# Sums of squares for the norms: four tiles added on GpSimd before TensorE sums the partitions, and a last block that ends tile by tile

## The chip, the cores and the metric

One core of a Trainium2 chip runs the whole program. The metric is device time in microseconds (us) of one execution; a lower number is better. The engines are named as in the profile: PE (TensorE), DVE (VectorE), ACT (ScalarE), POOL (GpSimd), SP (which issues DMAs).

## What is computed

The reference is two transformer blocks over 256 tokens of width 1024, all in fp32. The first mixes by grouped-query attention and a long convolution and then runs a product-key mixture of experts; the second group has four feed-forward blocks, two attentions (one differential, one with forget gates) and a key/value stage. What matters here is the norm that stands ahead of each stage:

```python
def rmsnorm(x, g):
    xf = x.astype(jnp.float32)
    y = xf * lax.rsqrt(jnp.mean(xf * xf, axis=-1, keepdims=True) + EPS)
    return (y * g.astype(jnp.float32)).astype(x.dtype)
```

The result of the last block goes through one more such norm, and that is the output.

## The kernel before

The activations stay in SBUF transposed: X is eight tiles of 128 features x 256 tokens in fp32, features on the partitions. Weights come from HBM as 427 loads of 1 MB, called raw, issued by SP into a ring of five buffers (three in the early stages). Each raw holds two units of 128 x 1024. ACT copies a unit to a reduced format (whi, about 1.06 us) and DVE subtracts to get the rest (wlo, about 1.22 us); the split units stand in a second ring of five buffers (LOOK + 1 = 3 in the early stages, XLOOK = 2 more later). PE multiplies a unit by the hi and lo parts of the activations, 24 matmuls in all (hi x whi, hi x wlo, lo x whi for eight tiles).

The stages run in the order mix, peer, f00, diff, f01, kv, f10, forget, f11. A norm needs the sum of squares over the features, that is over tiles and partitions: ACT squares each of the eight tiles (sq), and PE multiplies each square by a matrix of ones and accumulates eight products in one PSUM tile, ss. These matmuls are fp32; each shows in the profile as two rows. ACT then takes the root (r0, with a table load ahead of it where the function on ACT changes) and DVE the reciprocal (rstd).

In the stages from peer on, `norm_begin` doesn't wait for rstd: it scales X by the gain alone (xg, hi parts on ACT and lo parts on DVE), PE multiplies the first units by xg (outputs qkv, gux, kvu, bq, wq), and `fixed` multiplies their PSUM results by rstd afterwards (fix, DVE). A unit's PSUM buffer is free only after its fix, so PE can run three units (u1, u2, u3 below) and has to wait with the fourth (u4) for the fix of u1. In f00 two norms are merged: that of the first part's end and that of f00. So ss has two halves there; the second is weighted with the square of the gain `fin` (tile fsq).

`rstd` is the plain form, used twice in mix (for X and for the context). `finish` is the end of f11: eight updates of X by DVE, a square of each (six on ACT, two on DVE), eight ss matmuls, root, reciprocal, eight products, four output DMAs. Ahead of it `out_tiles` multiplies the last two pairs of f11 into eight output tiles, held in four PSUM tiles acc0 to acc3.

Python order, priorities and a list scheduler set the order of each engine's instructions when the program is built; on the chip each engine runs its list in order and waits at an instruction until its inputs are there. GpSimd has little to do: fills, index patterns and five DMA issues, among them that of scr<-vec, a 1.5 MB scatter of a bias table to HBM in f00 (`diff_setup`: PE's bv, ACT's vec, then POOL's DMA).

Everything is recorded by one helper, so that the profile shows nearly all instructions at L263; tiles tell them apart.

Of the kernel before, what the change touches and what calls it, by code (L numbers as in the profile page):

```python
# [9 lines left out]
F32 = mybir.dt.float32  # L10
# [117 lines left out]
PACE = {"route": {"v": 1}, "kv_norm": {"v": 2}}  # L128
NOSYNC = mybir.DependencyInfo(mybir.DependencyClass.NoSync, mybir.DependencyReason.DATA)
# [152 lines left out]
class Kern:  # L282
# [160 lines left out]
    def rstd(self, x, pool, n=D, tag="rstd"):  # L443
# [5 lines left out]
        for kt in range(nk):  # L449
            sq = pool.tile([P, T], F32, tag="sq", name="sq", bufs=3)  # L450
            nc.scalar.activation(sq, x[:, kt], AF.Square)
            nc.tensor.matmul(ps, self.ones, sq, start=kt == 0, stop=kt == nk - 1)
# [4 lines left out]
        return o  # L457

# [9 lines left out]
    def norm_begin(self, pool, G, sh, xg, fin=None, psq=None):  # L468
# [22 lines left out]
        fsq = None  # L491
        if fin is not None:
            fsq = pool.tile([P, KT], F32, tag="fsq", name="fsq", bufs=1)
            nc.vector.tensor_mul(fsq, fin, fin)
        for kt in range(KT):
            sq = (psq or pool).tile([P, T], F32, tag="sq", name="sq", bufs=8 if psq else 4)
            nc.scalar.activation(sq, x[:, kt], AF.Square)
            for j in range(n):
                w = fsq[:, kt:kt + 1].to_broadcast([P, P]) if j else self.ones
                nc.tensor.matmul(ps[:, j], w, sq, start=kt == 0 and j == 0, stop=kt == KT - 1, skip_group_check=n > 1)  # L500
# [65 lines left out]
    def ffn(self, ph, l, i):  # L566
# [7 lines left out]
        with ExitStack() as es:  # L574
# [20 lines left out]

            def out_tiles():
                ws = [S.take(ph, self.ffn_order("o", f)) for f, _, _ in pend]
                self.rows(acc, [(f, w, (ah, al)) for w, (f, ah, al) in zip(ws, pend)], NF)
                pend.clear()
                self.tick()  # L600

            for f in range(NF):
# [38 lines left out]
                pend.append((f, ah, al))  # L641
            out_tiles()
# [3 lines left out]
            if ph == "f11":  # L646
                self.finish(pa, pn, parts, half)
            else:
                self.add_x(parts, half)
# [12 lines left out]
    def finish(self, psq, pool, parts, g):  # L662

        nc = self.nc
        ps = self.ps_bg.tile([P, T], F32, tag="bg", name="ss")
        for kt, p in enumerate(parts):
# [3 lines left out]
            if kt < 6:  # L670
                nc.scalar.activation(sq, x, AF.Square)
            else:
                nc.vector.tensor_mul(sq, x, x)
            if kt == 5:
                nc.scalar.activation(pool.tile([P, 1], F32, tag="sqw", name="sqw", bufs=1), self.eps, AF.Sqrt)
            nc.tensor.matmul(ps, self.ones, sq, start=kt == 0, stop=kt == KT - 1)
# [1354 lines left out]
```

## Time and profile before

| what | value |
|---|---|
| median of 3 runs | 2221.97 us (2220.69 to 2222.41) |
| profiled execution | 2221.92 us, span 2220.1 us |
| PE / DVE / ACT / POOL busy | 98% / 77% / 52% / 0% of the span |
| granted TensorE clock, mean | 0.995 |
| chain that ended last | PE 86%, DVE 8%, ACT 3%, DMA 3% |
| matmuls into ss | 88, shown as 176 rows |

The span is what the profiler saw of the program; 1.8 us of the execution lie around it. The chain is followed back from the last instruction to what released each, so its shares say which engine the end of the program hangs on.

### The profile page before, as it was taken

Reading aid. Unit: us, or ns where it says so; the run is one execution under the profiler, and the core shown is the slowest. Engines: PE = TensorE matmul, PEld = TensorE weight load, DVE = VectorE, ACT = ScalarE, POOL = GpSimd, SP = SyncE. Lnnn points to the kernel's source line nnn. Section 1 sums busy time; section 2 is a strip of 40 time slices with the busy share of each in tenths; the row PEclk is TensorE's granted clock in tenths of the full one; section 3 lists DMA queues with packets and bytes.
Section 4 is the critical chain, followed back from the end, with each engine's and each line's share of the span. In section 5 each row is a group of like instructions: output and inputs, shape, how many; then the busy total and the mean of one; then the engine's idle time right before and its main releaser. Section 6 shows DMA issues by size and latency. Waiting matters only on the chain.

```text
span 2220.1 us, 41653 instructions
## 1 busy us (share of the span) xinstructions
PE 2176.8 (98%) x17298; PEld 2091.2 (94%) x17298; DVE 1706.2 (77%) x3056; ACT 1150.0 (52%) x1788; POOL 10.9 (0%) x25
## 2 busy tenths in 40 slices
PE   7999999999999999999999899999999999999998
PEld 4887999999889999999999899999999999999998
DVE  7789689887996777567777687878776887798554
ACT  5677565454334444444455345766445544476443
POOL 0000000000000000000000000000000000000000
PEclk9999999999999999999999999999999999999999
DMA  8256344544349888557776875436784688724551
GB/s 317 77 188 221 126 180 152 190 176 185 124 152 274 303 304 297 198 204 271 291 286 193 323 307 225 146 141 225 299 305 165 228 323 313 273 96 171 190 180 49
DMA packets 100605, 481.20 MB, mean 217 GB/s; under 512 B 40808, under 2 KB 41336, under 8 KB 44928
## 3 DMA queue, kind: packets, MB, share of 16 engines
q1 hardware_dynamic: 95744, 462.70, 57.4%
q10 hardware_dynamic: 3456, 10.90, 1.3%
q0 software_dynamic: 1216, 4.94, 1.0%
q8 instruction: 136, 2.23, 0.4%
q14 instruction: 53, 0.43, 0.1%
HBM read 467.48 MB, written 11.03 MB: 216 GB/s over the span
## 4 chain that ended last, share of the span: by engine, by line
PE 86%; DVE 8%; ACT 3%; DMA 3%; issue 1%; SPq 0%; DVEq 0%; ACTq 0%
PE acc L263 27%; PE gu L263 19%; PE u L263 15%; PE win L263 4%; DMA raw<-wts 3%; PE qkv L263 2%; PE gux L263 2%; DVE wlo L263 2%; PE pacc L263 2%; PE kvu L263 2%; PE gps L263 2%; PE ss L263 2%; PE sc L263 1%; DVE A L263 1%; PE po L263 1%; ACT whi L263 1%
## 5 line engine op out<-in xcount | busy, mean ns | idle before, releaser
L263 DVE TENSOR_TENSOR wlo<-raw,whi 128x1024 fp32r<-128x1024 f32 x650 | 792.6, 1222 | 302.8 <-ACT whi L263 301.0
L263 ACT ACTIVATE whi<-raw 128x1024 fp32r<-128x1024 f32 x650 | 684.3, 1055 | 498.2 <-PE acc L263 128.1
L263 PE MATMUL gu<-hh,wlo 128*128 128x256 f32 x1264 | 309.9, 283 | 0.0
L263 PE MATMUL gu<-hh,whi 128*128 128x256 f32 x1264 | 309.8, 283 | 0.0
L263 PE MATMUL acc<-wh,whi 128*128 128x256 f32 x1024 | 289.8, 283 | 0.0
L263 PE MATMUL acc<-wh,wlo 128*128 128x256 f32 x1024 | 289.8, 283 | 0.0
L263 PE MATMUL acc<-wl,whi 128*128 128x256 f32 x1024 | 289.8, 283 | 0.0
L263 DVE SCALAR_TENSOR_TENSOR junk<-raw,crow 128x1024 f32<-128x1024 f32 x198 | 241.7, 1220 | 47.4 <-DMA raw<-wts 38.6
L263 PE MATMUL u<-hh,whi 128*128 128x256 f32 x1024 | 253.7, 284 | 3.4 <-ACT whi L263 3.4
L263 PE MATMUL u<-hh,wlo 128*128 128x256 f32 x1024 | 253.1, 285 | 2.1 <-DVE wlo L263 2.1
L263 PEld LDWEIGHTS gu<-hh,whi 128*128 128x128 f32 x1264 | 241.5, 191 | 0.0
L263 PEld LDWEIGHTS gu<-hh,wlo 128*128 128x128 f32 x1264 | 241.5, 191 | 0.0
L263 PE MATMUL acc<-ah,whi 128*128 128x256 f32 x704 | 198.5, 282 | 6.7 <-ACT ah L263 6.7
L263 PEld LDWEIGHTS u<-hh,whi 128*128 128x128 f32 x1024 | 196.4, 192 | 5.1 <-ACT whi L263 5.1
L263 PEld LDWEIGHTS u<-hh,wlo 128*128 128x128 f32 x1024 | 196.2, 192 | 5.2 <-DVE wlo L263 4.0
L263 PE MATMUL acc<-al,whi 128*128 128x256 f32 x704 | 198.7, 283 | 0.8 <-DVE al L263 0.8
L263 PE MATMUL acc<-ah,wlo 128*128 128x256 f32 x704 | 197.0, 280 | 0.0
L263 PEld LDWEIGHTS acc<-wh,whi 128*128 128x128 f32 x1024 | 196.6, 192 | 0.0
L263 PEld LDWEIGHTS acc<-wh,wlo 128*128 128x128 f32 x1024 | 196.6, 192 | 0.0
L263 PEld LDWEIGHTS acc<-wl,whi 128*128 128x128 f32 x1024 | 196.6, 192 | 0.0
L263 PE MATMUL gu<-hl,whi 128*128 128x256 f32 x1264 | 177.4, 283 | 0.0
L263 PEld LDWEIGHTS gu<-hl,whi 128*128 128x128 f32 x1264 | 163.0, 191 | 0.0
(393 smaller groups left out, 4034.2 us busy)
## 6 DMA issues: line engine op xcount, KB each, us to landing
raw<-wts SPq DMA_DIRECT2D x427, 1024.0 KB, 4.9
G<-sp ACTq DMA_DIRECT2D x16, 512.0 KB, 2.6
gl<-G SPq DMA_DIRECT2D x16, 512.0 KB, 7.0
Fb<-fscr POOLq DMA_DIRECT2D x1, 2048.0 KB, 9.5
scr<-vec POOLq DMA_DIRECT2D x1, 1536.0 KB, 36.9
KR<-wts SPq DMA_DIRECT2D x1, 1024.0 KB, 11.1
KS<-wts SPq DMA_DIRECT2D x1, 1024.0 KB, 12.8
X<-xT SPq DMA_DIRECT2D x1, 1024.0 KB, 14.8
```

What stands on the lines that cost most here:

```text
L263: i = f(*a, **kw)
```

## The change

The sum of squares gets a method of its own, `sumsq`. ACT squares the eight tiles as before. GpSimd adds pairs of squares and then the two sums, so that four tiles become one in three additions, and PE multiplies only that one by the ones: two matmuls for eight tiles and six additions on GpSimd, where eight matmuls stood. It is used by both calls of `rstd` (four buffers for squares instead of three) and by `norm_begin` (five instead of four). In f00 the second half of ss has eight squares of its own, taken by ACT with the gain as a scale, and fsq goes. Over the program 60 matmuls go, 60 additions on GpSimd and eight squares on ACT come.

The second part concerns the end of f11: `out_last` multiplies both remaining pairs into one output tile, then both into the next, and `finish` becomes a generator that updates X two tiles at a time behind them and issues the ss matmuls of a pair of tiles after the next pair. There all eight ss matmuls stay on PE.

```diff
--- before.py
+++ after.py
@@ -126,6 +126,8 @@
 CH = 4
 
 PACE = {"route": {"v": 1}, "kv_norm": {"v": 2}}
+
+SQB = 5
 NOSYNC = mybir.DependencyInfo(mybir.DependencyClass.NoSync, mybir.DependencyReason.DATA)
 ASTEPS, HSTEPS = 1.5, 1
 RRATE = 60
@@ -446,15 +448,26 @@
         ps = self.ps_bg.tile([P, T], F32, tag="bg", name="ss")
         nk = n // P
         nc.scalar.activation(pool.tile([P, 1], F32, tag="sqw", name="sqw"), self.eps, AF.Sqrt)
-        for kt in range(nk):
-            sq = pool.tile([P, T], F32, tag="sq", name="sq", bufs=3)
-            nc.scalar.activation(sq, x[:, kt], AF.Square)
-            nc.tensor.matmul(ps, self.ones, sq, start=kt == 0, stop=kt == nk - 1)
+        self.sumsq(pool, ps, x, nk)
         r = pool.tile([P, T], F32, tag="r0", name="r0", bufs=1)
         nc.scalar.activation(r, ps, AF.Sqrt, scale=1.0 / n, bias=self.eps)
         o = pool.tile([P, T], F32, tag=tag, name=tag)
         nc.vector.reciprocal(o, r)
         return o
+
+    def sumsq(self, pool, ps, x, nk=KT, start=True, scale=None, bufs=4, **kw):
+
+        nc = self.nc
+        sq = []
+        for kt in range(nk):
+            t = pool.tile([P, T], F32, tag="sq", name="sq", bufs=bufs)
+            nc.scalar.activation(t, x[:, kt], AF.Square, scale=1.0 if scale is None else scale[:, kt:kt + 1])
+            sq.append(t)
+            if kt % 2:
+                nc.gpsimd.tensor_add(sq[kt - 1], sq[kt - 1], t)
+            if kt % 4 == 3:
+                nc.gpsimd.tensor_add(sq[kt - 3], sq[kt - 3], sq[kt - 1])
+                nc.tensor.matmul(ps, self.ones, sq[kt - 3], start=start and kt == 3, stop=kt == nk - 1, **kw)
 
     def mod_args(self, sh, sc, g, i=0):
         self.S.flush_ada([sh, sc])
@@ -488,16 +501,9 @@
                 nc.scalar.activation(hi[:, kt, :T], x[:, kt], AF.Copy, scale=Gx[:, kt:kt + 1])
                 nc.vector.scalar_tensor_tensor(lo[:, kt, :T], x[:, kt], Gx[:, kt:kt + 1], hi[:, kt, :T],
                                                op0=ALU.mult, op1=ALU.subtract)
-        fsq = None
-        if fin is not None:
-            fsq = pool.tile([P, KT], F32, tag="fsq", name="fsq", bufs=1)
-            nc.vector.tensor_mul(fsq, fin, fin)
-        for kt in range(KT):
-            sq = (psq or pool).tile([P, T], F32, tag="sq", name="sq", bufs=8 if psq else 4)
-            nc.scalar.activation(sq, x[:, kt], AF.Square)
-            for j in range(n):
-                w = fsq[:, kt:kt + 1].to_broadcast([P, P]) if j else self.ones
-                nc.tensor.matmul(ps[:, j], w, sq, start=kt == 0 and j == 0, stop=kt == KT - 1, skip_group_check=n > 1)
+        for j in range(n):
+            self.sumsq(psq or pool, ps[:, j], x, start=j == 0, scale=fin if j else None, bufs=8 if psq else SQB,
+                       skip_group_check=n > 1)
         r = pool.tile([P, T], F32, tag="rstd", name="rstd", bufs=1)
         r0 = pool.tile([P, T], F32, tag="r0", name="r0", bufs=1)
         with self.tc.high_priority(offset=NPRIO):
@@ -592,6 +598,20 @@
                     nc.vector.scalar_tensor_tensor(self.X[:, kt], self.X[:, kt], fin[:, kt:kt + 1], rf,
                                                    op0=ALU.mult, op1=ALU.mult)
                     yield
+
+            def out_last():
+
+                ws = [S.take(ph, self.ffn_order("o", f)) for f, _, _ in pend]
+                fin = self.finish(pa, pn, [acc[o // 2][:, o % 2] for o in range(8)], self.half(self.ada_done[mods[2]]))
+                for o in range(8):
+                    s = slice(o * P, (o + 1) * P)
+                    for w, (f, ah, al) in zip(ws, pend):
+                        self.mm_unit(acc[o // 2][:, o % 2], (w[0][:, s], w[1][:, s]), (ah, al), kts=range(1),
+                                     start=False, stop=f == NF - 1, skip_group_check=True)
+                    if o % 2:
+                        next(fin)
+                for _ in fin:
+                    pass
 
             def out_tiles():
                 ws = [S.take(ph, self.ffn_order("o", f)) for f, _, _ in pend]
@@ -639,14 +659,15 @@
                 if pend and f < NF - 1:
                     out_tiles()
                 pend.append((f, ah, al))
+            if ph == "f11":
+                assert mods[2] in self.ada_done
+                out_last()
+                return
             out_tiles()
             S.flush_ada(mods[2:]) if mods[2] not in self.ada_done else None
             self.mark("ffn.fin")
             parts, half = [acc[o // 2][:, o % 2] for o in range(8)], self.half(self.ada_done[mods[2]])
-            if ph == "f11":
-                self.finish(pa, pn, parts, half)
-            else:
-                self.add_x(parts, half)
+            self.add_x(parts, half)
 
     @staticmethod
     def ffn_order(kind, f):
@@ -663,6 +684,11 @@
 
         nc = self.nc
         ps = self.ps_bg.tile([P, T], F32, tag="bg", name="ss")
+        sqs = []
+
+        def ss(kt):
+            nc.tensor.matmul(ps, self.ones, sqs[kt], start=kt == 0, stop=kt == KT - 1)
+
         for kt, p in enumerate(parts):
             x = self.X[:, kt]
             nc.vector.scalar_tensor_tensor(x, p, g[:, kt:kt + 1], x, op0=ALU.mult, op1=ALU.add)
@@ -671,9 +697,15 @@
                 nc.scalar.activation(sq, x, AF.Square)
             else:
                 nc.vector.tensor_mul(sq, x, x)
+            sqs.append(sq)
             if kt == 5:
                 nc.scalar.activation(pool.tile([P, 1], F32, tag="sqw", name="sqw", bufs=1), self.eps, AF.Sqrt)
-            nc.tensor.matmul(ps, self.ones, sq, start=kt == 0, stop=kt == KT - 1)
+            if kt % 2:
+                for k in range(kt - 3, kt - 1) if kt >= 3 else ():
+                    ss(k)
+                yield
+        ss(KT - 2)
+        ss(KT - 1)
         r0 = pool.tile([P, T], F32, tag="r0", name="r0", bufs=1)
         nc.scalar.activation(r0, ps, AF.Sqrt, scale=1.0 / D, bias=self.eps)
         r = pool.tile([P, T], F32, tag="rstd", name="rstd", bufs=1)
```

Where the lists of the engines change most, with buffer numbers in the names:

First ACT at the norm of f00, before: splits of units (whi), the root r0, and rf, a second root that is used later.

```order
834 L263 ACTIVATE whi_13251<-raw_13042 128x1024
835 L263 ACTIVATE whi_13285<-raw_13042 128x1024
836 L263 ACTIVATE r0_13220<-ms2_13223 128x256
837 L263 ACTIVATE whi_13335<-raw_13105 128x1024
838 L263 ACTIVATE rf_13582<-ms_13221 128x256
839 L263 ACT_TABLE_LOAD
```

And after, from the last of the sixteen squares on (cols_76 holds the gain):

```order
843 L265 ACTIVATE sq_13228<-X_80,cols_76 128x256
844 L265 ACTIVATE whi_13265<-raw_13042 128x1024
845 L265 ACTIVATE whi_13299<-raw_13042 128x1024
846 L265 ACTIVATE whi_13349<-raw_13105 128x1024
847 L265 ACTIVATE whi_13391<-raw_13105 128x1024
848 L265 ACTIVATE r0_13234<-ms2_13237 128x256
849 L265 ACTIVATE vec_13480<-bv_13478 8x384
```

Two more splits stand ahead of r0, the fourth of them being whi_13391; vec, which scr's DMA waits for, has moved from behind several later instructions to the place after r0.

Second PE at the norm of diff, before: six of the eight ss matmuls stand together inside the first unit, qkv_15635 (x8 are its lo products); qkv_15672 is u2.

```order
8961 L263 MATMUL qkv_15635<-xg0_13152,wlo_15429 128x258
8962 L263 MATMUL ss_15569<-sq_15594,ones_78 128x256
8963 L263 MATMUL ss_15569<-sq_15597,ones_78 128x256
8964 L263 MATMUL ss_15569<-sq_15600,ones_78 128x256
8965 L263 MATMUL ss_15569<-sq_15603,ones_78 128x256
8966 L263 MATMUL ss_15569<-sq_15606,ones_78 128x256
8967 L263 MATMUL ss_15569<-sq_15609,ones_78 128x256
8968 L263 MATMUL qkv_15635<-xg1_13153,whi_15428 128x258 x8
8969 L263 MATMUL qkv_15672<-xg0_13152,whi_15456 128x258
```

And after, where qkv_15649 is u1 and qkv_15686 is u2 (whi_15470 and wlo_15471 come from the same raw as those of u1). The first ss stands after 31 products of the two units, the second after 38, with ten of u2 behind it:

```order
8955 L265 MATMUL qkv_15686<-xg0_13152,whi_15470 128x258
8956 L265 MATMUL ss_15583<-sq_15602,ones_78 128x256
8957 L265 MATMUL qkv_15649<-xg1_13153,whi_15442 128x258 x3
8958 L265 MATMUL qkv_15686<-xg0_13152,wlo_15471 128x258
8959 L265 MATMUL qkv_15686<-xg0_13152,whi_15470 128x258
8960 L265 MATMUL qkv_15686<-xg0_13152,wlo_15471 128x258
8961 L265 MATMUL qkv_15649<-xg1_13153,whi_15442 128x258
8962 L265 MATMUL ss_15583<-sq_15614,ones_78 128x256
8963 L265 MATMUL qkv_15686<-xg0_13152,whi_15470 128x258
8964 L265 MATMUL qkv_15686<-xg0_13152,wlo_15471 128x258
8965 L265 MATMUL qkv_15686<-xg1_13153,whi_15470 128x258 x8
8966 L265 MATMUL qkv_15721<-xg0_13152,whi_15506 128x258
```

The two units are interleaved now, and the two ss stand within them, each waiting for GpSimd.

Third ACT at the norm of diff, before and after. From the third square on before:

```order
962 L263 ACTIVATE sq_15594<-X_80 128x256
963 L263 ACTIVATE sq_15597<-X_80 128x256
964 L263 ACTIVATE sq_15600<-X_80 128x256
965 L263 ACTIVATE sq_15603<-X_80 128x256
966 L263 ACTIVATE sq_15606<-X_80 128x256
967 L263 ACTIVATE sq_15609<-X_80 128x256
968 L263 ACTIVATE whi_15631<-raw_15268 128x1024
969 L263 ACT_TABLE_LOAD
970 L263 ACTIVATE r0_15613<-ss_15569,eps_83 128x256
971 L263 ACTIVATE whi_15666<-raw_15268 128x1024
```

From the fifth square on after:

```order
974 L265 ACTIVATE sq_15614<-X_80 128x256
975 L265 ACTIVATE sq_15616<-X_80 128x256
976 L265 ACTIVATE sq_15619<-X_80 128x256
977 L265 ACTIVATE sq_15621<-X_80 128x256
978 L265 ACTIVATE whi_15645<-raw_15282 128x1024
979 L265 ACTIVATE whi_15680<-raw_15282 128x1024
980 L265 ACT_TABLE_LOAD
981 L265 ACTIVATE r0_15627<-ss_15583,eps_83 128x256
982 L265 ACTIVATE whi_15717<-raw_15349 128x1024
```

Both splits of the next raw now stand ahead of the table load and r0. On DVE, behind r0 in both orders, come the reciprocal, one wlo and the fix of u1.

## Rows read from the trace of the kernel before

**Rows 1.** The page, part 1: busy time of each engine over the span.

```profile
PE 2176.8 (98%) x17298; PEld 2091.2 (94%) x17298; DVE 1706.2 (77%) x3056; ACT 1150.0 (52%) x1788; POOL 10.9 (0%) x25
```

**Rows 2.** Windows: length, busy us (instructions) by engine, PE clock, DMA share, GB/s.

```profile
40.00:60.00 20.00, 18.31 (x118) 16.46 (x117) 19.44 (x41) 13.28 (x24) 0.00 (x0) 0.91 0.70 265
...
320.00:340.00 20.00, 20.00 (x171) 20.00 (x170) 20.00 (x85) 12.17 (x21) 0.00 (x0) 1.00 0.44 158
...
1520.00:1540.00 20.00, 20.00 (x170) 20.00 (x170) 18.50 (x33) 10.44 (x15) 0.00 (x0) 1.00 0.77 285
```

**Rows 3.** Chain that ended last, in order of time: start, us, what.

```profile
1177.73 9.95 PE gux L263 x81
...
1379.91 2.59 PE ss L263 x12
...
1382.50 7.10 PE qkv L263 x59
...
1506.27 10.09 PE gux L263 x84
...
2207.78 3.47 PE ss L263 x16
...
2211.27 0.48 ACT r L263
```

**Rows 4.** GpSimd by line and shape: busy us, mean ns of one, idle before.

```profile
L1576 POOL IOTA iota<- 128x256 f16 x1 | 1.5, 1527 | 1.7 <-DVE hl L263 1.7
...
L1252 POOL MEMSET kz<- 128x1024 f32 x1 | 1.0, 952 | 0.3 <-POOLq L2013 0.3
...
L1118 POOL IOTA tau<- 128x256 f32 x1 | 0.3, 345 | 0.1
```

**Rows 5.** Timeline of ScalarE at the norm of diff: start, us, what, idle before.

```profile
1379.13 2.09 ACT L263 ACTIVATE sq<-X 128x256 f32<-128x256 f32 x6
...
1382.19 1.28 ACT L263 ACT_TABLE_LOAD   x1
...
1383.48 0.47 ACT L263 ACTIVATE r<-ss,eps 128x256 f32<-128x256 f32 x1
```

**Rows 6.** Timeline of VectorE in the same stretch.

```profile
1377.93 3.25 DVE L263 SCALAR_TENSOR_TENSOR xg<-X,gcol,xg 128x256 fp32r<-128x256 f32 x8
...
1381.10 2.35 DVE L263 TENSOR_TENSOR wlo<-raw,whi 128x1024 fp32r<-128x1024 f32 x2
...
1383.99 1.75 DVE L263 RECIPROCAL rstd<-r 128x256 f32<-128x256 f32 x1 [0.33 <-ACT r L263]
...
1386.74 0.41 DVE L263 TENSOR_TENSOR fix<-qkv,rstd 128x256 f32<-128x256 f32 x1
```

**Rows 7.** Timeline of ScalarE at the norm of f00.

```profile
1170.92 2.24 ACT L263 ACTIVATE sq<-X 128x256 f32<-128x256 f32 x7
...
1178.84 1.06 ACT L263 ACTIVATE whi<-raw 128x1024 fp32r<-128x1024 f32 x1 [4.73 <-PE gux L263]
...
1179.81 0.40 ACT L263 ACTIVATE r<-ms 128x256 f32<-128x256 f32 x1
...
1190.56 0.46 ACT L263 ACTIVATE vec<-bv 8x384 f32<-8x384 f32 x1
```

**Rows 8.** Timeline of VectorE in the same stretch.

```profile
1181.08 1.74 DVE L263 RECIPROCAL rstd<-r 128x256 f32<-128x256 f32 x1
...
1184.00 0.75 DVE L263 TENSOR_TENSOR fix<-gux,rstd 128x256 f32<-128x256 f32 x2
```

**Rows 9.** Windows behind the start of f00, columns as in rows 2.

```profile
1185.00:1191.00 6.00, 6.00 (x47) 5.22 (x46) 6.00 (x16) 5.26 (x11) 0.00 (x0) 1.00 0.04 16
...
1221.00:1230.00 9.00, 2.93 (x20) 2.43 (x19) 4.36 (x8) 1.19 (x3) 0.93 (x1) 0.85 0.49 149
...
1230.00:1236.00 6.00, 6.00 (x36) 6.00 (x37) 5.78 (x10) 2.35 (x4) 0.00 (x0) 0.66 0.96 361
```

**Rows 10.** The page, part 6: DMA issues, KB each, us to landing.

```profile
scr<-vec POOLq DMA_DIRECT2D x1, 1536.0 KB, 36.9
```

## The prediction

> **What bounds the kernel.** The page's busy times come first: PE is busy for 2176.8 of 2220.1 us [rows 1], so what is taken off PE's list can shorten the run, if nothing else ends last at that place. The windows say where that holds. In the feed-forward stages PE is busy for 20.00 us of 20, with DVE at 18.50 or less; in the first half of peer DVE is full too (20.00), and in mix DVE has 19.44 of 20 where PE has 18.31 [rows 2]. So PE's time is worth its full price only behind the norms of f00, f01, kv, forget and f11, about half of it or less elsewhere, and at each norm the question is whether PE then waits for the squares' sum, the reciprocal or the fix.
>
> **What goes.** One ss matmul costs PE 0.43 us (2.59 us for six, 3.47 us for eight at the end) [rows 3]. The 60 that go are 25.9 us, twelve in f00 (5.2 us) and six, or 2.6 us, at each of eight other norms. This is the ceiling of the gain, 1.2% of the run.
>
> **What comes.** No row shows a GpSimd addition. The nearest are its fills and index patterns of one output and no SBUF input: 345 ns for 128x256 fp32 from below; 1527 ns for 128x256 with another type from above [rows 4]. The fill of 128x1024 in 952 ns is some 0.9 ns an element and stream; three streams (two in, one out) of 256 elements at that are 0.71 us. I take 0.7 us for an addition: it moves data as the fill does, while the slowest row converts types. The ends, 0.35 and 1.53 us, stay for the range. Three additions in a row are then 2.1 us where PE spent 1.7 us on four matmuls, so the sum of squares is finished later than the squares allow, and it is later than before unless it had been PE that was late.
>
> **The norm of diff, as the pattern.** Products cost 7.10/59 = 0.120 us each. At 1382.50 PE had eight of u1 left, so u2 ended at 1382.50 + 32 x 0.120 = 1386.35 and u3 at 1389.2 [rows 3]. The six last squares run from 1379.13, one every 0.32 us [rows 5]. With the change the first four are there at 1379.85; with the first pair already summed, two additions end at 1381.25, and the first ss follows. The eighth square takes the buffer of an addend and waits for that addition, until 1381.65. The other three additions run from 1381.25 to 1383.35, the second ss ends at 1383.8, and ten products are behind it: u2 ends at 1385.0, a gain of 1.3 of the 2.6 us. Up to there PE has enough to do, since the lo parts of xg arrive until 1381.2 [rows 6]. The root loses, though: two splits of 1.05 us now stand ahead of the table load, so that ACT has 1381.65 + 2.1 + 1.3 = 1385.05 and the root ends at 1385.5 instead of 1383.95 [rows 5]. Behind it come the reciprocal (1.75), one wlo (1.16) and the fix (0.4) [rows 6]: 1388.9. But u3 now ends at 1387.9, and u4 waits 1.0 us. Of 2.6 us, **0.3** are left in diff. In forget the list is the same: 0.3. In f01 no table load precedes the root, and before it PE had run all four units without a stop (84 products in 10.09 us [rows 3]); in kv one split only stands ahead of the root and no wlo between reciprocal and fix: there I keep the 1.2 us. f11 has two splits and the load, but earlier squares: 0.7. The five sum to **-3.7 us**. With additions of 0.35 us the second ss in diff ends near 1382.4 and the fix near 1388.4: the five give -8.3. With 1.53 us the second ss ends at 1388.0 and u2 at 1389.2, 2.9 us later than before: five times that is +14.5.
>
> **The norm of f00.** Sixteen squares follow one another from 1170.9 on, the last ends near 1175.8 [rows 7]; twelve additions of 0.7 us from 1171.3 on end at 1179.7. Then the last ss (0.43) and 24 products: u3 ends at 1183.1. Before, 57 of the 81 products behind 1177.73 take it to 1184.7 [rows 3]. So 1.6 of 5.2 us are left. But r0 now stands behind four splits. The fifth buffer of the split ring serves the first; the others wait for u1, u2 and u3, as the split at 1178.84 waited for PE's u1 [rows 7]. So r0 starts only after u3 has ended and the fourth split is made (1.06), while DVE does that unit's wlo (1.2) ahead of the reciprocal (1.74) and the fix (0.4) [rows 7, 8]: u4 starts at 1183.1 + 4.5 = 1187.6, against 1184.7, where the fix of 1184.00 was there in time [rows 8]. This is **+2.9 us** (+0.6 with the fast addition, whose u3 ends at 1180.7).
>
> **What this does to the transfer behind it.** scr's DMA hangs on vec, which was at 1190.56 [rows 7] behind bv and comes right after r0 now, at 1184.6: 5.9 us earlier. The DMA engines were nearly idle then (share 0.04, 16 GB/s, from 1185 to 1191). Later they are what PE waits for: of the 9 us from 1221 on PE has 2.93 busy, 6.1 are idle, and over the next 6 us the granted clock has a mean of 0.66, between its two levels of 1.2 and 2.4 GHz, so that another 2.0 us go [rows 9]. scr takes 36.9 us, through all of that stretch [rows 10], and holds up the weights. On GpSimd its issue stands behind the twelve additions, which are over by 1179.7, and the next additions, those of diff, are 180 us away. If it starts 5.9 us earlier in an idle time while PE's demand comes 2.9 us later, the wait of 8.1 us could all but go; since weights and scr share the engines, I count **-6.0 us** (bounds 0 and -8).
>
> **The rest.** Mix: for X the transfers of the first weights bound, 0; for the context DVE bounds [rows 2], and all eight squares now stand ahead of ACT's evictions, paced by GpSimd: **+0.5** (0 to +3). Peer: DVE bounds what follows, PE starts earlier but the root is later: **-0.3** (-1 to +1). Tail: PE did 48 products and eight ss without a gap and r0 followed at 2211.27 [rows 3]; it does the same work now, but four ss are ahead of the last products, so that the last products end at 2207.78 + 1.7 = 2209.5, the last two updates and squares (DVE, four of 0.4) at 2211.2, one more ss at 2211.65: **+0.4** (0 to +0.8).
>
> Sum: -3.7 + 2.9 - 6.0 + 0.5 - 0.3 + 0.4 = -6.2 us against the profiled execution of 2221.92 us, which stands at the median of 2221.97: **2216 us**.
>
> **A rule that speaks against it.** In diff DVE runs without a gap from 1377.93 to 1383.45, with xg's lo parts (X and the hi part in) and wlo (raw and whi in) [rows 6]; no row of this trace has a GpSimd instruction that reads SBUF beside such work. The Trainium skill ("SBUF — State Buffer", section Who interferes with whom) says that a DVE instruction with two SBUF inputs and a GpSimd instruction that reads SBUF exclude each other for a whole instruction. No run here shows it yet; by that rule the time would be that of rival 3 below, instead of the 2216 us of the sum.
>
> **The rivals.**
> 1. *Additions are fast* (0.35 us) and PE keeps its gain: -8.3 (five norms) + 0.6 - 7 (f00 and scr) - 0.8 (peer) + 0.4 (tail) = -15, **2207 us**. For it: GpSimd's pattern of the same shape takes 345 ns. Against: it reads nothing.
> 2. *The transfer behind f00 is no shorter*: the stall moves with scr instead of shrinking. The sum without its -6.0 is -0.2, **2222 us**. For it: the raw loads have the same ring and nearly the same order as before.
> 3. *DVE and GpSimd hinder one another*, and the change is slower. In diff six additions push DVE's row of xg and three wlo (6.75 us from 1377.93) by 4.2 us to 1388.9; reciprocal, wlo and fix end at 1392.2, u4 is 3 us late. Over the five norms +12, in mix's context, where DVE bounds, +4.2, in f00 DVE comes 5 us later, of which scr's stall gives back most (+2), peer +1, tail +0.4: +20, **2242 us**. The 26 us between this and the sum come from 0.7 us of lost DVE time an addition; from some 0.17 us on the gain is gone, from 0.3 the change is slower. With half the loss it is near 2230.
>
> **The numbers.** My forecast has 0.40, with 2210 to 2220 as its own range; rival 1 0.18, rival 2 0.20, rival 3 0.22. A measurement of this kernel can tell about 0.2%, 4.4 us, from no change. The forecast (nearly all) and rival 1 are faster: 0.55. Rival 2 and the edges of forecast and rival 3 are the same: 0.24. The rest of rival 3 is slower: 0.21. The range, 2205 to 2236, leaves out the lower part of rival 1 and the upper half of rival 3.
>
> **What will show it.** GpSimd additions near 0.7 us and, if rival 3 is right, xg or wlo rows on DVE with gaps or lengthened beside them; at diff u2 ending 1.3 us sooner after the last product of acc, r0 1.5 us later, and PE waiting about 1 us ahead of u4; at f00 PE idle for nearly 4 us after u3, with r0 behind four splits; scr issued before its old place and less PE idle 40 us later. I am wrong first of all if additions are far from 0.7 us, if the idle time in f00 itself takes the clock down as the later one did (some 2 us), or if the stall stays.

## The result and the profile after

The changed kernel is slower: 2252.64 us (median of 4 runs, 2251.67 to 2256.56) against 2221.48 us (2220.69 to 2222.41), a ratio of 1.0145 [1.013, 1.0159]. Times are medians of fast executions; one of e9's ten below took 3475 us at a granted clock of 0.56 and is left out. The prediction of 2216 us, its range (up to 2236) and its sign are wrong.

The page after, part 1, busy time of each engine over the span of 2251.3 us, answers to [rows 1]:

```profile
PE 2173.4 (97%) x17178; PEld 2083.4 (93%) x17178; DVE 1720.2 (76%) x3055; ACT 1154.4 (51%) x1796; POOL 72.9 (3%) x85
```

The 120 rows of 60 matmuls are gone, 25.9 us at the 0.43 us of [rows 3], yet PE is busy only 3.4 us less. The other 22.5 us are for the most part the same products at a lower clock (its mean is 0.986, it was 0.995; 2150.9 x 0.995 / 0.986 is 2170.5 us, which is 19.6 of them). And PE's idle time, span less busy, has grown from 43.3 to 77.9 us: -25.9 + 22.5 + 34.6 = +31.2 us, which is the growth of the span.

What the idle time ends with is in the waits of PE after (us in total, times, longest). The kernel before has no such waits of ss or gux. The last row answers to one of the kernel before that had 6.7 us, 5.8 of them in the idle stretch of [rows 9]; it stands first here:

```profile
PE acc L263 <- ACT ah L263: 6.7, 2, 5.8
...
PE ss L265 <- POOL sq L469: 23.8, 13, 4.8
PE gux L265 <- DVE fix L265: 4.5, 2, 2.7
...
PE acc L265 <- ACT ah L265: 1.5, 2, 1.0
```

GpSimd by line and shape after (busy us, mean ns of one, idle before); L467 adds two squares, L469 adds the two sums, and A is the tile of peer. They answer to [rows 4], where no addition was to be had:

```profile
L467 POOL TENSOR_TENSOR sq<-sq 128x256 f32<-128x256 f32 x36 | 39.2, 1102 | 781.2 <-ACT sq L265 705.9 <-DVE xg L265 75.2
L469 POOL TENSOR_TENSOR sq<-sq 128x256 f32<-128x256 f32 x18 | 17.5, 970 | 1.4
...
L469 POOL TENSOR_TENSOR A<-A 128x256 f32<-128x256 f32 x2 | 1.5, 734 | 0.2
```

An addition that has SBUF to itself takes 0.73 us, as the two of A do; the means of 1.10 and 0.97 are those of additions beside VectorE. Three timelines show what happens (start, us, what, idle before). GpSimd first, at mix, f00, diff, f01 and f11; the first line is scr's issue in the kernel before:

```profile
1191.33 1.10 POOL L703 DMA_DIRECT2D scr<-vec  x1 [21.34 <-ACT vec L263]
...
23.01 1.58 POOL L469 TENSOR_TENSOR sq<-sq 128x256 f32<-128x256 f32 x1
...
1180.68 4.22 POOL L467 TENSOR_TENSOR sq<-sq 128x256 f32<-128x256 f32 x2 [1.42 <-ACT sq L265]
1184.98 0.72 POOL L469 TENSOR_TENSOR sq<-sq 128x256 f32<-128x256 f32 x1
...
1199.63 1.10 POOL L735 DMA_DIRECT2D scr<-vec  x1 [6.40 <-ACT vec L265]
...
1392.30 0.79 POOL L469 TENSOR_TENSOR sq<-sq 128x256 f32<-128x256 f32 x1
1393.05 1.79 POOL L467 TENSOR_TENSOR sq<-sq 128x256 f32<-128x256 f32 x2
...
1516.84 3.38 POOL L467 TENSOR_TENSOR sq<-sq 128x256 f32<-128x256 f32 x2
...
2042.33 3.55 POOL L467 TENSOR_TENSOR sq<-sq 128x256 f32<-128x256 f32 x2 [75.24 <-DVE xg L265]
```

VectorE in the same places:

```profile
19.47 1.23 DVE L265 SCALAR_TENSOR_TENSOR junk<-KR,crow 128x1024 f32<-128x1024 f32 x1
...
20.73 1.62 DVE L265 SCALAR_TENSOR_TENSOR junk<-KR,zs 128x1024 f32<-128x1024 f32 x1
...
22.40 1.62 DVE L265 SCALAR_TENSOR_TENSOR junk<-KR,crow 128x1024 f32<-128x1024 f32 x1
...
1179.26 3.25 DVE L265 SCALAR_TENSOR_TENSOR xg<-X,gcolx,xg 128x256 fp32r<-128x256 f32 x8
1182.42 1.22 DVE L265 TENSOR_TENSOR wlo<-raw,whi 128x1024 fp32r<-128x1024 f32 x1
...
1389.48 5.64 DVE L265 SCALAR_TENSOR_TENSOR xg<-X,gcol,xg 128x256 fp32r<-128x256 f32 x8
1395.04 1.75 DVE L265 TENSOR_TENSOR wlo<-raw,whi 128x1024 fp32r<-128x1024 f32 x1
...
1517.99 3.31 DVE L265 TENSOR_TENSOR wlo<-raw,whi 128x1024 fp32r<-128x1024 f32 x2
```

And TensorE:

```profile
1185.76 1.08 PE L265 MATMUL ss<-sq,ones 128*128 128x256 f32 x2 [4.00 <-POOL sq L469]
...
1193.29 0.70 PE L265 MATMUL ss<-sq,ones 128*128 128x256 f32 x2 [1.26 <-POOL sq L469]
...
1201.48 0.55 PE L265 MATMUL gux<-xg,whi 128*128 128x258 f32 x1 [2.67 <-DVE fix L265]
...
1393.14 0.70 PE L265 MATMUL ss<-sq,ones 128*128 128x256 f32 x2 [0.71 <-POOL sq L469]
1395.76 0.70 PE L265 MATMUL ss<-sq,ones 128*128 128x256 f32 x2 [0.20 <-POOL sq L469]
...
1521.94 1.22 PE L265 MATMUL ss<-sq,ones 128*128 128x256 f32 x2 [3.46 <-POOL sq L469]
```

The reader is to see two forms of one thing. In mix, and at diff, VectorE and GpSimd take turns: VectorE's instruction goes from 1.23 to 1.62 us beside an addition of 1.58; xg's eight lo parts take 5.64 us instead of 3.25 [rows 6]. At f00 VectorE runs its row undisturbed (3.25 us for xg's eight, as at diff before [rows 6]), and it is GpSimd that stands: two additions begun at 1180.68 end at 1184.9, 1.3 us after VectorE's row at 1183.6. Alone they take 1.41. At f11 the pair takes 3.55 us in the same way. At f01 both engines lose: the pair takes 3.38 us, and the two wlo beside it 3.31 us instead of some 2.4. TensorE, which runs its list in order, stands at the ss that needs them, 4.00, 3.46 and 2.93 us. After such a stop the same two rows of ss take 1.08 to 1.22 us instead of 0.70: the clock has fallen.

Windows after, columns as in [rows 2]; the first two answer to the norm of f00 and to the idle stretch of [rows 9], the third is the norm of f01, and the fourth the four us behind its long wait:

```profile
1185.00:1205.00 20.00, 14.17 (x76) 12.62 (x77) 12.33 (x19) 12.05 (x20) 9.10 (x11) 0.78 0.46 161
1232.00:1257.00 25.00, 22.84 (x185) 22.03 (x184) 14.89 (x24) 9.57 (x13) 0.92 (x1) 1.00 0.90 341
1515.00:1535.00 20.00, 15.50 (x101) 14.64 (x100) 15.40 (x25) 10.29 (x18) 6.52 (x5) 0.83 0.37 127
...
1522.00:1526.00 4.00, 4.00 (x17) 3.82 (x18) 1.77 (x2) 0.49 (x2) 0.00 (x0) 0.50 0.77 279
```

The stretch that PE stood in before is filled now (22.84 of 25 us at the full clock), while two norms, where PE was the bound, have a quarter of their time idle and a mean clock near 0.8. Behind the wait of f01 TensorE runs at 0.50, the lower of its two levels.

The shift of VectorE's first update of X in a stage (after less before) gives the loss by stage. The sum by the prediction stands beside it:

| stretch | ends with | before, us | after, us | shift | of this stretch | predicted |
|---|---|---|---|---|---|---|
| mix, peer | X at f00 | 1166.85 | 1176.11 | +9.3 | +9.3 | +0.2 |
| f00 | X by rf | 1203.72 | 1221.32 | +17.6 | +8.3 | +2.9 |
| rest of f00 | X at diff | 1374.79 | 1386.33 | +11.5 | -6.1 | -6.0 |
| diff, f01 | X at kv | 1691.84 | 1709.11 | +17.3 | +5.7 | -1.5 |
| kv, f10 | X at forget | 1938.56 | 1957.72 | +19.2 | +1.9 | -1.2 |
| forget | X at f11 | 2012.37 | 2036.86 | +24.5 | +5.3 | -0.3 |
| f11, tail | the end of the span | 2220.1 | 2251.3 | +31.2 | +6.7 | -0.3 |

The first row also holds what executions differ by: in the five kernels that leave mix and peer as they were (before, e1, e8, e9, e10), X at f00 stands between 1165.59 and 1172.07 us, largely by one wait in mix for a DMA (hf, 1.1 to 7.4 us). That noise is mix's: peer took 887.2 us before and 891.3 after, so +4.1 of the row are peer's (+2.8 in e2, which has the same sums).

### The profile page after: what moved, and what is told of

It reads as the page before. It is cut to its first block, busy times and chain, and to the rows that moved or that the text cites. A ratio compares the mean times of both kernels' runs of the same rounds, so it can differ in the third digit from the quotient of the medians.

```text
span 2251.3 us, 41499 instructions
## 1 busy us (share of the span) xinstructions
PE 2173.4 (97%) x17178; PEld 2083.4 (93%) x17178; DVE 1720.2 (76%) x3055; ACT 1154.4 (51%) x1796; POOL 72.9 (3%) x85
## 4 chain that ended last, share of the span: by engine, by line
PE 86%; DVE 6%; ACT 3%; POOL 2%; DMA 2%; issue 1%; SPq 0%; DVEq 0%; POOLq 0%; ACTq 0%
PE acc L265 26%; PE gu L265 19%; PE u L265 16%; PE win L265 4%; PE qkv L265 2%; DVE wlo L265 2%; PE pacc L265 2%; PE kvu L265 2%; PE gps L265 2%; PE sc L265 2%; PE gux L265 2%; POOL sq L467 1%; DMA raw<-wts 1%; PE po L265 1%; ACT whi L265 1%; PE outs L265 1%
## 6 DMA issues: line engine op xcount, KB each, us to landing
X<-xT SPq DMA_DIRECT2D x1, 1024.0 KB, 14.9
```

## The experiments

Two theories stood against each other. **Chain**: squares, additions one behind the other, ss, root, reciprocal and fix are now longer than the work that PE has meanwhile, so PE waits at each norm, whoever adds; the clock that falls in the wait makes it worse. **Exclusion** (rival 3): VectorE loses its time to GpSimd. The letters e1 to e10 number the kernels; those on record say "the change" for the changed kernel.

**e1: the new end of f11 alone**, on the kernel before.

```diff
+            if ph == "f11":
+                assert mods[2] in self.ada_done
+                out_last()
+                return
...
-            nc.tensor.matmul(ps, self.ones, sq, start=kt == 0, stop=kt == KT - 1)
+            if kt % 2:
+                for k in range(kt - 3, kt - 1) if kt >= 3 else ():
+                    ss(k)
+                yield
```

> The kernel before with the new end of f11 alone. In the trace of the change the start of the last X updates was 29.4 us late and the end of the run 31.2 us, so about 1.8 us should belong to this part: 2223 us if it is independent of the rest. The step of the prediction (+0.4) would give 2222. Both theories of the sums (exclusion of GpSimd and DVE; a chain of additions in front of an in-order PE) leave it there.

2222.53 us, ratio 1.0001 [0.9991, 1.0011]. The last entries of its chain (start, us, what), which answer to the end of [rows 3]:

```profile
2207.93 1.07 PE acc L263 x9
...
2209.02 0.88 DVE X L263 x2
2209.90 0.34 DVE sq L263
...
2210.29 1.15 PE ss L263 x4
...
2211.45 0.48 ACT r L263
```

The root starts at 2211.45 where it was 2211.27. PE's eight ss no longer stand in a row at the end; two updates, a square and two ss (2.4 us from 2209.02 to 2211.43) have their place. By the medians the second part of the change moves nothing that can be measured. Within a profiled run it costs a little: from the first update of X at f11 to the end of the span e1 takes 208.96 us where the kernel before takes 207.73.

**e2: the additions alone**, with the end of f11 as before.

```diff
...
-            for j in range(n):
-                w = fsq[:, kt:kt + 1].to_broadcast([P, P]) if j else self.ones
-                nc.tensor.matmul(ps[:, j], w, sq, start=kt == 0 and j == 0, stop=kt == KT - 1, skip_group_check=n > 1)
+        for j in range(n):
+            self.sumsq(psq or pool, ps[:, j], x, start=j == 0, scale=fin if j else None, bufs=8 if psq else SQB,
+                       skip_group_check=n > 1)
```

> The additions on GpSimd everywhere, but the end of f11 as before. If the two parts add up, 2252.6 - 1.8 = 2250.8 us; both theories say so. Under 2240 would mean that the two parts hurt each other.

2249.41 us, ratio 1.0123 [1.0106, 1.014]: nearly the whole loss lies in the additions.

**e3: the same sums, added on VectorE**, so that no addition excludes anything.

```diff
-                nc.gpsimd.tensor_add(sq[kt - 1], sq[kt - 1], t)
+                nc.vector.tensor_add(sq[kt - 1], sq[kt - 1], t)
...
-                nc.gpsimd.tensor_add(sq[kt - 3], sq[kt - 3], sq[kt - 1])
+                nc.vector.tensor_add(sq[kt - 3], sq[kt - 3], sq[kt - 1])
```

> The change with its 60 additions on DVE instead of GpSimd. Theory exclusion (an addition on GpSimd takes 0.72 us alone and up to 4.2 us beside DVE's instructions with two SBUF inputs, and these are stretched too): an addition costs about 0.35 us on DVE and nothing is blocked, so most of PE's 25.7 us of waiting for the sums and the fall of the clock go: 2215 to 2232 us. Theory chain (any chain of squares and additions ahead of PE's in-order list makes PE wait): the waits stay nearly as they are, 2240 us or more.

2246.73 us, ratio 1.0104 [1.0085, 1.0122]. Waits of PE in e3:

```profile
PE gux L265 <- DVE fix L265: 10.6, 3, 3.8
PE ss L265 <- DVE sq L265: 9.4, 4, 5.8
...
PE bq L265 <- DVE fix L265: 3.0, 1, 3.0
PE qkv L265 <- DVE fix L265: 3.0, 1, 3.0
```

An addition costs VectorE 0.416 us (54 of them 20.8 us), GpSimd has none, and nearly the same is lost; now the fix is late more often than ss. (The 4.2 us of the expectation are those of two additions.) The loss doesn't need the exclusion. VectorE's own time for the additions is part of it here, so this run alone doesn't show that the rest is the chain.

**e5: the exclusion without the chain.** The kernel before, with all products on PE, and as many additions on GpSimd whose result nobody reads.

```diff
+            sqs.append(sq)
+            self.shadow(pool, sqs)
...
+        if kt % 2:
+            d = pool.tile([P, T], F32, tag="sqd", name="sqd", bufs=1)
+            nc.gpsimd.tensor_add(d, sq[kt - 1], sq[kt])
+            if kt % 4 == 3:
+                nc.gpsimd.tensor_add(d, d, sq[kt])
```

> The kernel before, with the same number of additions of squares on GpSimd, whose results nobody reads; all eight products for ss stay on PE. Theory exclusion in its strong form (DVE loses the time of the additions, and that is the loss): in the norm of diff the eight xg of DVE take 5.6 us instead of 3.25, and the run ends at 2232 to 2245 us. Theory chain: nobody waits for an addition, 2220 to 2226 us, whatever DVE's rows show.

2230.79 us, ratio 1.004 [1.0026, 1.0054]: +8.4 us, between the two. VectorE in e5 at diff, and GpSimd at f01:

```profile
1381.20 5.69 DVE L263 SCALAR_TENSOR_TENSOR xg<-X,gcol,xg 128x256 fp32r<-128x256 f32 x8
...
1511.04 3.28 POOL L467 TENSOR_TENSOR sqd<-sq 128x256 f32<-128x256 f32 x2
```

The exclusion is there, 5.69 us for xg and 3.28 for the pair of f01, close to the 5.64 and 3.38 of the changed kernel, and costs 8.4 us over the program. PE waits for no addition; only through the squares' buffers, which an addition keeps longer, does anything hang on GpSimd (ss waits 1.1 us for squares in mix). The changed kernel has the same exclusion and 25.9 us less to do on PE, which would make 8.4 - 25.9 = -17.5 us if PE's time were worth its full price and nothing else had changed; it loses 31. What it has beyond e5 is that PE waits for what GpSimd adds, and lists in another order.

**e8: the additions in diff, f01, kv, forget and f11 alone.**

```diff
...
-        for kt in range(KT):
+        if fin is None and not isinstance(pool, SubPool):
+            self.sumsq(pool, ps[:, 0], x, bufs=5)
+        for kt in range(KT if fin is not None or isinstance(pool, SubPool) else 0):
```

> The additions on GpSimd in diff, f01, kv, forget and f11 alone; mix, peer, f00 and the end as before. From the times of the X updates in the trace of the change these five lost 29.4 - 11.5 = 17.9 us: 2240 us if each norm's loss is its own. My prediction had a gain of 3.7 us there. Clearly less than 2235 would mean that these norms lose because of what mix and f00 did to the transfers ahead of them.

2240.79 us, ratio 1.0076 [1.0059, 1.0092]: these five cost 18.6 us, where the prediction had -3.7.

The traces tell where. A stage is taken here from its first update of X to that of the next, in the profiled run; left as it was, it agrees within 0.1 us between kernels (f01 194.10, 194.13 and 194.13 us in before, e1 and e9). The other columns are differences to before:

| stage | before, us | changed kernel | e8 | e5 | predicted |
|---|---|---|---|---|---|
| diff | 122.96 | -0.2 | +0.5 | +2.2 | -0.3 |
| f01 | 194.10 | +5.9 | +3.9 | 0.0 | -1.2 |
| kv, f10 | 246.72 | +1.9 | +5.8 | +0.7 | -1.2 |
| forget | 73.81 | +5.3 | +4.1 | +2.2 | -0.3 |
| f11 | 193.32 | +4.9 | +5.3 | 0.0 | -0.7 |
| sum | | +17.8 | +19.6 | +5.0 | -3.7 |

In f01 and f11 additions that nobody waits for (e5) cost nothing, though the pair at f01 is held up there as well. The loss of these two comes in with PE's waiting: its idle time grows by 5.3 and 4.8 us there, nearly all of it at ss and ahead of the fix. Forget is another matter: at its norm PE waits 0.72 and 0.20 us for ss, as in diff, and yet the stage is 5.3 us longer. PE's list is in another order through the whole stage there (93 of its bq products stand ahead of the first sc where 64 did, and 36 pacc behind the last po where 48 did). Its last 8.8 us, after and before, are these (columns as in [rows 2]):

```profile
2028.00:2036.80 8.80, 6.71 (x43) 5.37 (x42) 4.07 (x9) 2.04 (x5) 0.00 (x0) 0.81 0.33 122
...
2003.57:2012.37 8.80, 8.80 (x76) 8.37 (x75) 4.89 (x9) 3.53 (x8) 0.00 (x0) 1.00 0.67 241
```

How much of forget's loss the order makes and how much the later fix was not tried.

**e9: the additions in f00 alone.**

```diff
         if fin is not None:
-            fsq = pool.tile([P, KT], F32, tag="fsq", name="fsq", bufs=1)
-            nc.vector.tensor_mul(fsq, fin, fin)
-        for kt in range(KT):
+            for j in range(n):
+                self.sumsq(psq or pool, ps[:, j], x, start=j == 0, scale=fin if j else None, bufs=8 if psq else 5,
+                           skip_group_check=n > 1)
+        for kt in range(KT if fin is None else 0):
```

> The additions in f00's two merged norms alone (12 additions, 12 fewer matmuls; everything else as before). In the change f00 was 8.5 us late and the stall behind it gave 6.1 us back. Theory: the stall gives back because TensorE arrives late there, whoever made it late, so f00's own lateness of 8.5 us is what it takes back: 2222 + 8.5 - 6 = 2224.5 (2222 to 2227). Rival: it gave back the 9.3 us that were lost ahead of f00, and f00's own loss stays: 2230.

2225.82 us, ratio 1.0014 [1.0004, 1.0024]. PE stands 4.0 us at ss and 2.7 us ahead of the fix, as in the changed kernel, and in the stretch behind, the wait of acc for ah has gone from 6.7 to 0.7 us. From X's update to X by rf e9 is 7.7 us longer than before (44.5 against 36.9), to X at diff only 2.0 (209.9 against 207.9). So f00's loss is real, and the stall behind takes most of it back, whatever was lost earlier. With e8 and e2 this leaves some 5 us for mix and peer (27.0 less 18.6 less 3 to 4), of which the profiles give peer 2.8 to 4.1.

**e7: pairs only.** Four ss for eight squares, one addition for each.

```diff
             if kt % 2:
                 nc.gpsimd.tensor_add(sq[kt - 1], sq[kt - 1], t)
-            if kt % 4 == 3:
-                nc.gpsimd.tensor_add(sq[kt - 3], sq[kt - 3], sq[kt - 1])
-                nc.tensor.matmul(ps, self.ones, sq[kt - 3], start=start and kt == 3, stop=kt == nk - 1, **kw)
+                nc.tensor.matmul(ps, self.ones, sq[kt - 1], start=start and kt == 1, stop=kt == nk - 1, **kw)
```

> The change with pairs only: GpSimd adds two squares, TensorE sums four such tiles (40 additions and 40 fewer matmuls instead of 60 and 60; 17.3 us of matmuls go instead of 25.9). Theory chain (squares, then additions one behind the other, then a TensorE that waits in order, and the clock that falls in the wait): the last square is followed by one addition instead of two, the waits of ss for GpSimd fall from 24 us to 10 to 14, and the time is 2230 to 2240. Theory exclusion (each addition costs VectorE its own length, nothing else): two thirds of the additions leave two thirds of the loss, 1/3 less gain: 2222 + 2/3 x 30 = 2242. If only the removed matmuls counted, it would be 2205.

2231.54 us, ratio 1.0053 [1.0035, 1.007]. Waits of PE in e7:

```profile
PE ss L265 <- POOL sq L467: 10.5, 11, 3.1
...
PE gux L265 <- DVE fix L265: 3.4, 2, 2.7
```

It takes less work off PE than the changed kernel (17.3 us instead of 25.9) and is 21 us faster, as a shorter chain should be; the waits for GpSimd fall from 23.8 to 10.5 us. Fewer additions also leave less for the exclusion to hold up, so e7 doesn't separate the two.

**e10: e8 with ss later in TensorE's list**, behind 20 to 35 more products.

```diff
-                nc.tensor.matmul(ps, self.ones, sq[kt - 3], start=start and kt == 3, stop=kt == nk - 1, **kw)
+                with self.tc.high_priority(offset=-100):
+                    nc.tensor.matmul(ps, self.ones, sq[kt - 3], start=start and kt == 3, stop=kt == nk - 1, **kw)
```

> The additions in diff, f01, kv, forget and f11 alone (that was 2240.8 us), with the two ss matmuls of a norm placed some 20 to 35 products later in TensorE's list. Theory place (TensorE loses because ss stands in its list ahead of work whose inputs are there): the waits of ss for GpSimd, 10.6 us, go to under 2 us and the time to 2226 to 2232. Theory length (the chain squares, additions, ss, root, reciprocal, fix has no slack in any place): the waits for GpSimd go and come back as waits of gux, qkv, bq and kvu for the fix, and the time is 2238 to 2248.

2242.19 us, ratio 1.0088 [1.0071, 1.0105]: nothing gained on e8. Waits of PE in e10:

```profile
PE gux L263 <- DVE fix L263: 11.7, 2, 6.8
...
PE ss L263 <- POOL sq L470: 1.1, 1, 1.1
```

In e8 the same two rows had 1.8 and 10.6 us. The wait has changed its name: at f01 2.2 us ahead of ss became 6.8 us ahead of the fourth unit. But the edit moved more than ss. At f01 four splits instead of two now stand ahead of the root, and VectorE's list reads:

```profile
1515.61 1.74 DVE L263 RECIPROCAL rstd<-r 128x256 f32<-128x256 f32 x1
1518.17 1.23 DVE L263 SCALAR_TENSOR_TENSOR junk<-raw,crow 128x1024 f32<-128x1024 f32 x1 [0.82 <-DMA raw<-wts]
...
1519.32 0.75 DVE L263 TENSOR_TENSOR fix<-gux,rstd 128x256 f32<-128x256 f32 x2
```

So the reciprocal starts 2.2 us later than in e8 (1513.37), and 2 us of the wait for the fix are a sum that waited for a transfer. At diff the first ss ran at 1386.92, 3.4 us after the last addition had ended. What e10 shows is that this place is no better than that of e8; it doesn't show that no place would be.

**e6: the changed kernel with 48 more products on PE**, two behind each second square of peer, diff, f01, kv, forget and f11, into the unused half of ss's tile. The kernel's result is not that of the reference (relative error 0.60), so only its time is read.

```diff
...
+            if fill is not None and kt % 2:
+                for _ in range(2):
+                    nc.tensor.matmul(fill, self.ones, t, start=True, stop=True, skip_group_check=True)
```

> The change, with eight more products per norm in peer, diff, f01, kv, forget and f11, of squares that are there anyway, into a half of the PSUM bank that nobody reads: 48 products, 20.6 us of PE's time. Theory chain with the clock (in these norms PE stands some 12 us for the sums, and the lower clock behind it costs about 14 more): the products fill the waits and hold the clock up, 2242 to 2250 us. If the granted clock is a side show, the added work shows where it doesn't fit into waits: 2258 us or more.

2249.42 us, ratio 1.0126 [1.011, 1.0143], so no slower than the changed kernel (the intervals overlap) with 20.6 us more for PE to do. The page of e6, part 1:

```profile
PE 2180.8 (97%) x17274; PEld 2088.8 (93%) x17274; DVE 1721.8 (77%) x3055; ACT 1155.5 (51%) x1796; POOL 72.2 (3%) x85
```

PE's busy time grows by 7.4 us only, since the mean clock is back at 0.994; the other 13.2 us of the added work are made up for by the clock, and the idle time falls from 77.9 to 66.0 us. The waits of ss for GpSimd stay (21.7 us, were 23.8). So this much work at the norms is free in the changed kernel, and with the mean clock back nearly all of the loss stays. What the full clock would give back without the added work isn't shown.

**e4: the products made cheaper instead of fewer.** The kernel before with squares and ones in fp32r, which needs one row of PE for a matmul where fp32 needs two; peer stays in fp32.

```diff
-            sq = (psq or pool).tile([P, T], F32, tag="sq", name="sq", bufs=8 if psq else 4)
+            sq = (psq or pool).tile([P, T], F32R, tag="sq", name="sq", bufs=8 if psq else 4)
...
-        self.ones = c.tile([P, P], F32, name="ones")
-        nc.vector.memset(self.ones, 1.0)
...
+        self.ones = c.tile([P, P], F32R, name="ones")
+        nc.vector.tensor_copy(self.ones, ones)
```

> The kernel before with its squares (except those of peer) and the ones written in the reduced fp32r format, so that the eight products per norm stay on PE but should cost 0.12 us each, as the products of the units do, instead of 0.43. Nobody waits for an addition, and the order is that of before. The squares are rounded in this kernel. If PE's time at the norms is worth its price, 80 products less by 0.31 us are up to 25 us: 2200 to 2212 us. If what follows a norm is bound by the root and the fix and not by PE, as both theories hold for the change, less than half of it stays: 2212 to 2220.

2207.27 us, ratio 0.993 [0.9913, 0.9946]: faster than both kernels. The page of e4, part 1:

```profile
PE 2159.7 (98%) x17218; PEld 2074.2 (94%) x17218; DVE 1704.8 (77%) x3057; ACT 1148.7 (52%) x1788; POOL 10.8 (0%) x25
```

PE is busy 17.1 us less than in [rows 1], and 14.9 us of it arrive in the time. The stages of its profiled run (12.2 us less in all) say where. Some 2.5 us (8 x 0.31) go at each norm, and 2.0 of them arrive in diff, 2.4 in f01, 2.2 in kv and f10 and 1.5 in f11; forget is 2.7 us longer. Another 5.6 us come in the stretch behind f00, whose wait of acc for ah falls from 6.7 to 1.3 us, as scr is issued 9.0 us earlier than before, with X by rf where it was (1203.59 us):

```profile
1182.31 1.09 POOL L703 DMA_DIRECT2D scr<-vec  x1 [11.36 <-ACT vec L263]
```

The premise of the prediction, that time taken off PE at the norms is worth nearly its full price, holds in three of these five stages as long as nothing is put into the chain; a good part of the total comes by the transfer and not by that price.

## Why the prediction was wrong, step by step

- **The price of an addition, "I take 0.7 us": right for one that runs alone** (0.72 to 0.74 us), and wrong for those that mattered. With VectorE's two-input work beside them they take 0.74 to 0.89 at diff, where VectorE is stretched, 1.58 to 1.70 in mix, and some 2 us each in the first pair of f00, 1.7 in that of f01 (4.22 and 3.38 for two).
- **The exclusion got a chance of 0.22, as a price that VectorE pays.** It exists: e5 puts it at 8.4 us where PE waits for no addition. But rival 3 let only VectorE's row slip. In f00, f01 and f11 it was GpSimd that stood, and with it ss. The Trainium skill ("SBUF — State Buffer", section Who interferes with whom) says that two such instructions exclude each other; the trace agrees that they do, while in mix a pair costs 1.67 us from start to start (20.73 to 22.40), less than the 1.23 + 0.72 = 1.95 of one after the other.
- **The five norms, -3.7, measured +18.6 (e8): the step that failed.** "In f01" and "in kv", where "I keep the 1.2 us", and the 0.7 of f11 were kept and not worked through; for f01 the sum rested on PE having run all four units without a stop before. That it had no wait then says that the chain fitted, not that it could be lengthened. An addition there took 1.7 us and not 0.7, PE stood 3.46 (f01) and 2.93 us (f11) at ss, and the stages became 5.9 and 4.9 us longer instead of 1.2 and 0.7 shorter; PE's idle time grew by 5.3 and 4.8 us in them, and e5, where nobody waits, lost nothing there. In diff, the one norm that was worked through in full, the rows are, from X on, up to 2 us later than forecast (ss waits of 0.71 and 0.20 us, the table load behind both splits, a fix at 1401.92), and the stage gained 0.2 us where 0.3 were forecast. "In forget the list is the same" held for the norm and not for the stage: its +5.3 us come with a new order up to its end, which the sum left out. e7 shows that the loss shrinks with the number of additions, e10 that the later place of ss doesn't bring it back.
- **f00, +2.9, measured +8.3 (7.7 in e9).** The mechanism was as told: r0 starts behind four splits, at 1197.98, and the fourth unit waits 2.67 us for the fix. What was missing is that the first two additions wait for VectorE's row of xg and wlo, so that ss holds PE for 4.00 us, ahead of products whose inputs are there.
- **The transfer behind f00, -6.0, measured -6.1: right in size and in kind, but its parts were off and made up for each other, which is luck.** The sum had scr 5.9 us earlier and PE's demand 2.9 later, 8.8 us more between the two. bv stands behind the held-up PE too, so that scr's issue, counted from the first update of X at f00, came 1.0 us earlier (23.52 us instead of 24.48), and X by rf came 8.3 later: 21.69 us lie between them where 12.39 did, 9.3 more. e9 gets there in the same way (21.02 us, a wait of 0.7), e4 by an earlier scr alone (21.28 us, 1.3); e8 leaves f00 as it was and keeps both (12.38 us, 6.9). Rival 2, that the stall stays, is out.
- **Mix and peer, +0.2, measured +9.3 in the profile and some 5 us by difference of runs.** "For X the transfers of the first weights bound, 0" is refuted: the additions run in step with the sums of VectorE there, PE stands 4.79 and 3.77 us at ss, and the first norm's reciprocal starts at 31.41 us instead of 28.39. Peer, -0.3, measured +2.8 to +4.1.
- **The tail, +0.4: no effect on the median, 1.2 us within the profiled run** (e1).
- **The clock.** The prediction names it last, as "some 2 us" in f00. In the changed kernel it is some 20 us of PE's busy time. In e6 the clock is back, with 20.6 us more of products, and nearly all of the loss is still there.

Rival 3 came nearest, 2242 us and slower, but its bill is not the one that was paid. Of the five norms' loss, 5.0 us are the additions' own price on VectorE by e5, all in diff, kv and forget. What stays open: how the rest divides between additions held up by VectorE and three additions in a row as such (moving VectorE's work away from them wasn't tried), what the new order of the lists costs by itself, and why the exclusion stretches VectorE at some norms and holds GpSimd at others. Kv shows both, with the first addition starting 0.6 us behind xg's row in either kernel: in the changed kernel ss waited 0.71 and 0.20 us there, in e8 once, for 3.6 us.

## What to carry to other kernels

An engine that is 98% busy doesn't make every instruction on its list worth its price: ask what the dependent chain behind it is (here squares, sum, root, reciprocal, fix) and whether the work that covers it has slack; a list without waits may only just fit it. Where a scheduler sets the lists, compare them for the whole stage and not only at the edit (forget). Work moved to an idle engine pays its own latency into that chain, and on GpSimd beside two-input work of VectorE a latency that can be three times what it is alone. Making the same instruction cheaper where it stands (fp32r, -14.9 us) beat moving it (+31).

## What the runs showed of the hardware

- A 128x256 fp32 addition with both inputs in SBUF takes GpSimd 0.72 to 0.74 us alone and VectorE 0.416 us. Beside VectorE instructions with two SBUF inputs the two either take turns (VectorE 1.23 to 1.62 us, GpSimd 1.58) or GpSimd stands until VectorE's row without a gap has ended (two additions in 4.22 us).
- The granted clock fell in PE's long waits: two rows of ss that take 0.70 us, also after a wait of 0.71, took 1.22 after one of 3.46 us, and from 1522 to 1526 us the clock was 0.50, the lower of the levels of 1.2 and 2.4 GHz. With dead products among the squares' sums (e6) the mean over the run was back at 0.994.
- The stall behind scr's transfer went with how far ahead of the demand it was issued: with 12.39 us between scr's issue and X by rf PE waited 6.7 us (acc for ah), with 19.40 us 3.1 (e3), with 21.02 us 0.7 (e9).
